# Transposing the small groups of the first head through VectorE and DRAM, with their scores further ahead

## The chip, the cores and the metric

The kernel runs on one core of a Trainium2 chip. The metric is the device time of one execution in microseconds (us); the kernel before takes 527.57 us, the median of three runs (525.86 to 528.05). The names of the engines in the rows are those of the profile: PE is TensorE's matmul side and PEld its weight load, DVE is VectorE, ACT is ScalarE, POOL is GpSimd, SP is SyncE (here only a DMA issuer; its queue is written SPq).

## The reference

One decoder layer on x of 1024 tokens by 1024 channels. Three mixers share one input projection: pooling, stick-breaking attention with 8 heads of 64, and softmax attention into 256 memory tokens. The change lies in the second:

```python
h = rmsnorm(x, norm_g)
proj = einsum('bsd,de->bse', h, w_in)          # pool_v, pool_gate, sb_q, sb_k, sb_v, sb_gate, mem_q, mem_gate
# stick-breaking attention, per head, for each block of 128 queries with L = the keys up to its end
z = einsum('bqhd,bkhd->bhqk', qb, kb) * scale
log_beta    = log_sigmoid(z)
log_1m_beta = where(mask, log_sigmoid(-z), 0)
cum  = cumsum(log_1m_beta, axis=-1)
a    = where(mask, exp(log_beta + cum[..., -1:] - cum), 0)
out  = einsum('bhqk,bkhd->bqhd', a, vb)        # then multiplied by silu(sb_gate)
# all groups concatenated, times w_out, plus x
```

## The kernel before, in words

Everything is computed in fp32 quality from products of high and low parts: an operand is rounded to a high part, the low part is the rest, and a product of two operands takes three matmuls (the calls that `unit_half` writes at L251 and L254). The projection is cut into units of 128 output channels: a unit is 16 steps of three 128x512 matmuls each. The units are the *fill*: matmuls that depend on nothing in the attention.

The stick-breaking attention is cut into 32 *groups* (p, j, h): p is one of four pairs of heads, j one of four stretches of 256 queries, and h the head of the pair, 0 (the first head) or 1. Group (p, j, h) sees 256(j+1) keys, that is 256, 512, 768 or 1024. Its keys are taken in j+1 *chunks* of 256; all groups make 80 chunks, numbered e = 0 to 79 in the order p, j, h. A pair of heads has 20 chunks.

For each group the kernel does this:

- `qk`: per block i of 128 queries, matmuls into a PSUM bank `z` (L754), a sigmoid on ACT into an SBUF tile `be` (L760, in pieces of up to 512 keys), then `scan`: a running product over the reversed row on DVE (L769). What comes out needs to be transposed, keys to partitions, before it can meet V.
- The transpose has two forms, chosen by `by_dma[n]`. Where it is false, `hl` calls `a_t`: four 128x128 transposes on PE into PSUM (L593, three for a group's last chunk, whose first half of the keys lies after the first 128 queries), the high part by ACT (L597) and the low part by DVE, which reads PSUM and the high part (L598). Where it is true, DVE transposes blocks of 32x32 in place right behind the scan (L771), four DMAs on SP's queue write the blocks to a DRAM tile `zd`, each block to its transposed place (L779), `rd` reads a chunk back three places ahead of its use (L799, or L804 and L805 for the last chunk of a group), and `hl` splits it: high part by ACT (L824), low part by POOL (L825), both from SBUF.
- `av`: four matmuls per chunk (L611) with the high and the low part against V, and at a group's end `av_out` on ACT (L630) and DVE (L633, L634).

Before the change the groups with h = 1 go through DRAM, and those with h = 0 through PE.

The order on every engine is written out by hand. `sb_slots` puts one `av` at each place e; at the same place stand `rd(e + 3)`, `hl(e + 1)` and the `qk` steps that a table gives. The scores of a couple of groups (p, j, 0) and (p, j, 1) are spread evenly over a window of places `c0` to `c1`, the second head first. `weave` then mixes the places with the fill in proportion, by planned PE times; `soon` puts an instruction that many planned microseconds later. The 80 places are cut in four parts, each woven with its own fill: the first with 48 fill steps and places up to e = 8, then e = 9 to 28, 29 to 48, and 49 to 79. The last part has 80 fill steps, and the pooling mixer's vector work (L927, L941 to L952) is written between them; the pooling needs DVE for its window sums and POOL for its low parts. This part is called the last stage below.

The `be` tiles rotate through four buffers, and for the first 58 tiles through two more (`Y0`, `Y1`). The tiles `al` have four buffers, `ah` two, and each PSUM bank name two.

Of the kernel before, what the change touches and what calls it, by code (L numbers as in the profile page):

```python
# [27 lines left out]
def layer_kernel(  # L28
# [707 lines left out]
    def sb_slots():  # L736
        groups = [(p, j, h) for p in range(4) for j in range(NT // 2) for h in range(2)]
        chunks = [(n, b) for n, (p, j, h) in enumerate(groups) for b in range(j + 1)]
        first = [chunks.index((n, 0)) for n in range(len(groups))]
        by_dma = [h == 1 for _, _, h in groups]  # L740
        be, zd, wt, acc, stored, n_be = {}, {}, {}, {}, [], [0]

        def qk(n, i, c):
# [99 lines left out]
        def qk_steps(n):  # L843
            p, j, h = groups[n]
            out = []
            for i in range(2):
                L = (2 * j + i + 1) * P
                for c in range((L - 1) // 512, -1, -1):
                    w = min(512, L - c * 512)
                    out.append((0.93e-3 * w, lambda i=i, c=c: qk(n, i, c)))  # L850
            return out


        slots = {}
        for n in range(0, len(groups), 2):
            c0, c1 = (first[n - 2] if n else -4) - 3, first[n] - 3
            for m, (lo, hi) in ((n + 1, (c0, (c0 + c1) / 2)), (n, ((c0 + c1) / 2, c1))):
                qs = qk_steps(m)
                for x, st in enumerate(qs):
                    slots.setdefault(int(lo + x * (hi - lo) / len(qs) // 1), []).append(st)  # L860
# [287 lines left out]
    def y_load():  # L1148
# [13 lines left out]
        )  # L1162
    )
    attn = sb_slots()
    weave(attn[0], fill_0)
    weave(attn[1], chain([u_q[2], u_k[2], u_g[2], u_v[2]], u_q[3]))
# [227 lines left out]
```

## Time and profile before

| what | value |
|---|---|
| median of 3 runs | 527.57 us (525.86 to 528.05) |
| profiled execution, its own time | 528.35 us |
| span in that profile, first to last instruction | 526.2 us |
| mean granted TensorE clock | 0.983 |
| PE busy | 499.3 us, 95% of the span |
| DVE busy | 403.4 us, 77% |
| ACT busy | 300.6 us, 57% |
| POOL busy | 248.2 us, 47% |

The first scores of the stick-breaking attention start on PE at 138.42 us, the last `av` matmuls at 419.76 us. From 437 us on the output projection runs. In a row of instructions in time order the columns are the start, the duration (of all merged instructions together, where xcount is above 1), engine, line, operation, and the tiles; behind them, in brackets, the idle time just before and what ended it. In the rows by groups the columns are the busy time, the mean of one instruction in ns, and the idle time before it. In the rows by stretches each engine has its busy time with the number of instructions, and then come the granted clock and the DMA engines' share.

### The profile page before, as it was taken

The page shows a single profiled execution, that of the slowest core. Times are in us where ns is not written, and L with a number is a line of the kernel's source. Part 1 is how long each engine was busy: PE and PEld are TensorE (multiplying, and loading weights), DVE is VectorE, ACT ScalarE, POOL GpSimd, SP SyncE. Part 2 cuts the span into 40 slices and gives each one's busy share as a digit, 9 for nine tenths or more (in the row PEclk, how much of TensorE's full clock was granted, in tenths as well). Part 3 has the DMA queues.
Part 4 walks back from the last instruction along what each step waited for, and adds up shares of the span by engine and source line. Part 5 has one row for each costly group of instructions (what it writes and reads, how often), then busy time and mean ns, then how long its engine had stood idle before and what let it go on. Part 6 is the DMA issues. An engine that isn't in the chain of part 4 may idle for free.

```text
span 526.2 us, 7899 instructions
## 1 busy us (share of the span) xinstructions
PE 499.3 (95%) x2548; PEld 416.4 (79%) x2548; DVE 403.4 (77%) x621; ACT 300.6 (57%) x676; POOL 248.2 (47%) x239
## 2 busy tenths in 40 slices
PE   7889999999999999999999999997878969999997
PEld 6678888888888788888888888885767848888886
DVE  4777777877379975699665998499993469999973
ACT  6877757778348654676556665564463438462400
POOL 4580335355124453544735348462474772055791
PEclk9999999999999999999999999998989978999999
DMA  8911111533537744665755756635445217323123
GB/s 308 333 40 41 30 52 40 119 85 79 127 80 154 152 101 107 149 131 116 146 125 148 141 123 140 150 70 130 124 87 159 80 53 229 120 81 124 35 105 135
DMA packets 150080, 62.45 MB, mean 119 GB/s; under 512 B 104070, under 2 KB 139160, under 8 KB 150040
## 3 DMA queue, kind: packets, MB, share of 16 engines
q1 hardware_dynamic: 150040, 61.96, 45.9%
q8 instruction: 20, 0.33, 0.3%
q14 instruction: 20, 0.16, 0.1%
HBM read 40.97 MB, written 16.78 MB: 110 GB/s over the span
## 4 chain that ended last, share of the span: by engine, by line
PE 70%; DVE 11%; ACT 6%; issue 4%; POOL 4%; DMA 3%; SPq 1%; DVEq 0%; POOLq 0%; ACTq 0%
PE av L611 6%; PE u_q L254 6%; PE u_k L254 5%; PE u_g L254 5%; DVE be L769 5%; PE u_v L254 4%; PE z L754 4%; PE u_q L251 3%; PE oS L1274 3%; PE oS L1276 3%; PE oS L1275 3%; PE u_k L251 3%; PE u_g L251 2%; PE u_pv L254 2%; PE oA L1274 2%
## 5 line engine op out<-in xcount | busy, mean ns | idle before, releaser
L769 DVE TENSOR_TENSOR_SCAN be<-be,later 128x128 f32<-128x128 f32 (+3 forms) x64 | 97.8, 1533 | 15.0 <-ACT be L760 14.8
L825 POOL TENSOR_TENSOR al<-al,ah 128x512 fp32r<-128x512 f32 (+1 forms) x40 | 61.4, 1537 | 44.0 <-ACT ah L824 40.2
L760 ACT ACTIVATE be<-z 128x128 f32<-128x128 f32 (+3 forms) x96 | 47.0, 491 | 41.7 <-PE z L754 31.1
L611 PE MATMUL av<-al,V_v 128*128 128x256 f32 (+1 forms) x160 | 32.8, 287 | 8.0 <-DVE al L598 6.1
L597 ACT ACTIVATE ah<-ta 128x512 fp32r<-128x512 f32 (+1 forms) x40 | 22.2, 554 | 30.7 <-PE ta L593 22.9
L598 DVE TENSOR_TENSOR al<-ta,ah 128x512 fp32r<-128x512 f32 (+1 forms) x40 | 25.2, 630 | 17.1 <-ACT ah L597 15.4
L611 PEld LDWEIGHTS av<-ah,V_v 128*128 128x128 f32 x160 | 29.9, 190 | 8.5 <-PE z L754 1.0
L611 PEld LDWEIGHTS av<-al,V_v 128*128 128x128 f32 x160 | 24.6, 192 | 9.5 <-DVE al L598 7.4
L611 PE MATMUL av<-ah,V_v 128*128 128x256 f32 (+1 forms) x160 | 30.5, 272 | 0.9 <-PE z L754 0.6
L703 POOL TENSOR_SCALAR pe_m<-pe_m,nb_m 128x256 f32<-128x256 f32 x16 | 16.8, 1053 | 27.8 <-DVE nb_m L700 24.1
L630 ACT ACTIVATE avt<-av,ve_v 64x128 f32<-64x128 f32 x64 | 19.8, 357 | 17.6 <-PE av L611 9.5
L754 PE MATMUL z<-KA_k,qa_q 128*128 128x512 f32 (+3 forms) x96 | 25.7, 352 | 2.7 <-ACT be L760 2.7
L824 ACT ACTIVATE ah<-al 128x512 fp32r<-128x512 f32 (+1 forms) x40 | 23.4, 584 | 6.8 <-DMA al<-zd 3.8
L251 PE MATMUL u_g<-hh,wh_g 128*128 128x512 f32 x64 | 26.5, 415 | 0.0
L251 PE MATMUL u_v<-hh,wh_v 128*128 128x512 f32 x64 | 26.3, 411 | 0.0
L251 PE MATMUL u_k<-hh,wh_k 128*128 128x512 f32 x64 | 26.2, 410 | 0.0
L1274 PE MATMUL oS<-bs,hh 128*128 128x512 f32 (+1 forms) x68 | 25.9, 380 | 0.0
L1276 PE MATMUL oS<-bs,hl 128*128 128x512 f32 (+1 forms) x68 | 25.8, 379 | 0.0
L771 DVE STREAM_TRANSPOSE be<-be 128x128 f32<-128x128 f32 (+7 forms) x32 | 24.9, 779 | 1.1
L754 PE MATMUL z<-KB_k,qb_q 128*128 128x512 f32 (+3 forms) x96 | 25.7, 350 | 0.0
L1275 PE MATMUL oS<-bs,hh 128*128 128x512 f32 (+1 forms) x68 | 25.6, 377 | 0.0
L692 ACT ACTIVATE pe_m<-z_m,nb_m,qsc 128x256 f32<-128x256 f32 x32 | 17.8, 561 | 13.5 <-DVE nb_m L688 11.0
(322 smaller groups left out, 1579.1 us busy)
## 6 DMA issues: line engine op xcount, KB each, us to landing
al<-zd SPq DMA_DIRECT2D x24, 256.0 KB, 2.9
x<-in_x_dram SPq DMA_DIRECT2D x8, 512.0 KB, 6.2
wr_q<-in_w_in_dram SPq DMA_DIRECT2D x4, 512.0 KB, 3.7
wr_k<-in_w_in_dram SPq DMA_DIRECT2D x4, 512.0 KB, 4.8
wr_v<-in_w_in_dram SPq DMA_DIRECT2D x4, 512.0 KB, 3.9
KA_k<-KA_k SPq DMA_DIRECT2D x8, 256.0 KB, 3.5
KB_k<-KB_k SPq DMA_DIRECT2D x8, 256.0 KB, 3.7
wr_g<-in_w_in_dram SPq DMA_DIRECT2D x4, 512.0 KB, 3.8
```

The source lines that it names most:

```text
L251: nc.tensor.matmul(pt[:], wh[:, kc], hh[k][:, c], start=(k == 0), stop=False)
L254: nc.tensor.matmul(pt[:], w[:, kc], h[k][:, c], start=False, stop=(k == KD - 1 and n == 1))
L598: low = lambda: nc.vector.tensor_tensor(al[:, :w], tp[:, :w], f(ah[:, :w]), op=ALU.subtract)
L611: nc.tensor.matmul(av[:, 256 - bw : 256], vs[n], part[:, o : o + bw], start=(first and part is ah and n == 0), stop=(last and part is al a ...
L754: nc.tensor.matmul(zp[:, 0:w], q[h][:, tcol], k[h][:, m, s0 : s0 + w], start=(m == 0), stop=(m == 1))
L760: nc.scalar.activation(t[:, s0 : s0 + w], zp[:, 0:w], AF.Sigmoid, scale=-(HD**-0.5))
L769: nc.vector.tensor_tensor_scan(t[:, rev], t[:, rev], mask, 1.0, op0=ALU.mult, op1=ALU.max)
L771: nc.vector.transpose(t[:, 0:L], t[:, 0:L])
L825: nc.gpsimd.tensor_tensor(lo[:, 0:w], f(lo[:, 0:w]), f(hi[:, 0:w]), op=ALU.subtract)
L1274: nc.tensor.matmul(bk[:, c], xh[:, tcol], wh[:, c], start=(n == 0), stop=False)
L1275: nc.tensor.matmul(bk[:, c], xh[:, tcol], wl[:, c], start=False, stop=False)
L1276: nc.tensor.matmul(bk[:, c], xl[:, tcol], wh[:, c], start=False, stop=(n == 3))
```

## The change

The groups of the first head with j = 0 and j = 1 (256 and 512 keys) now also have `by_dma` true. So that their stores reach DRAM before `rd` wants them, the scores of these couples end 6 places ahead of the group's first `av`, instead of 3. The windows now join: each begins where the one before it ends, so that the couple j = 0 has a window of 5 places instead of 8, j = 1 keeps 2, j = 2 has 7 instead of 4, and j = 3 keeps 6. The first of all begins at place -12 instead of -7, so that the first part is spread over 21 places instead of 16.

```diff
         first = [chunks.index((n, 0)) for n in range(len(groups))]
-        by_dma = [h == 1 for _, _, h in groups]
+        by_dma = [h == 1 or j < 2 for _, j, h in groups]
...
         slots = {}
+        c1 = -12
         for n in range(0, len(groups), 2):
-            c0, c1 = (first[n - 2] if n else -4) - 3, first[n] - 3
+            c0, c1 = c1, first[n] - (6 if by_dma[n] else 3)
             for m, (lo, hi) in ((n + 1, (c0, (c0 + c1) / 2)), (n, ((c0 + c1) / 2, c1))):
```

Eight groups change their form (two for each of the four pairs of heads), with 12 chunks. Behind the changed line the line numbers of the kernel are higher by one.

How the order moves, at three places of the last pair of heads. In the names, `be_3_1_2_0` is the score tile of pair 3, head 1, query block 2 (so j = 1); the last number is a buffer's. A line of "..." stands where rows are left out. First PE behind the `av` of chunk 60, where the transposes for chunk 62 stand, the first chunk of the first head's group of 512 keys. Before:

```order
L611 MATMUL av_41_4048<-al_60_3998,V_v3_3652 128x128
L251 MATMUL u_pg1_1_3946<-hh6_91,wh_pg1_3740 128x512
...
L754 MATMUL z_3_0_4_1_4064<-KA1_k3_3139,qa1_q3_2980 128x128 x2
L593 MATMUL ta_62_4069<-ident_69,be_3_0_2_0_3958 128x128
L593 MATMUL ta_62_4069<-ident_69,be_3_0_3_0_3973 128x128
...
L251 MATMUL u_pg1_1_3946<-hh7_92,wh_pg1_3740 128x512
```

And after the change, behind the same `av` of chunk 60:

```order
L611 MATMUL av_41_4130<-al_60_4000,V_v3_3689 128x128
L251 MATMUL u_pg1_1_4073<-hh5_90,wh_pg1_3789 128x512
L254 MATMUL u_pg1_1_4073<-hl5_98,wh_pg1_3789 128x512
L254 MATMUL u_pg1_1_4073<-hh5_90,wl_pg1_3790 128x512
L754 MATMUL z_3_0_5_0_4153<-KA1_k3_3233,qa1_q3_3015 128x512 x2
L251 MATMUL u_pg1_1_4073<-hh6_91,wh_pg1_3789 128x512
```

The transposes into `ta_62` are gone (two of its four are shown), and the scores at this point belong to a later query block; the fill around them is the same.

Second DVE in the same stretch, at the scores of j = 1 (query blocks 2 and 3); the scans (L769) are listed here under the name SCALAR_TENSOR_TENSOR. Before:

```order
L633 TENSOR_TENSOR av_39_3784<-av_39_3784,avt_2_0_3_3877 64x256
...
L927 TENSOR_TENSOR us1_3738<-us1_3738 128x511
...
L769 SCALAR_TENSOR_TENSOR be_3_1_2_0_3915<-be_3_1_2_0_3915,later_147 128x384
L771 STREAM_TRANSPOSE be_3_1_2_0_3915<-be_3_1_2_0_3915 128x384
...
L769 SCALAR_TENSOR_TENSOR be_3_1_3_0_3937<-be_3_1_3_0_3937,later_147 128x512
...
L769 SCALAR_TENSOR_TENSOR be_3_0_2_0_3958<-be_3_0_2_0_3958,later_147 128x384
L769 SCALAR_TENSOR_TENSOR be_3_0_3_0_3973<-be_3_0_3_0_3973,later_147 128x512
...
L598 TENSOR_TENSOR al_60_3998<-ta_60_3993,ah_60_3997 128x384
L769 SCALAR_TENSOR_TENSOR be_3_1_4_1_3991<-be_3_1_4_1_3991,later_147 128x640
```

And now:

```order
L769 SCALAR_TENSOR_TENSOR be_3_1_2_0_3882<-be_3_1_2_0_3882,later_147 128x384
...
L769 SCALAR_TENSOR_TENSOR be_3_1_3_0_3906<-be_3_1_3_0_3906,later_147 128x512
...
L769 SCALAR_TENSOR_TENSOR be_3_0_2_0_3925<-be_3_0_2_0_3925,later_147 128x384
L771 STREAM_TRANSPOSE be_3_0_2_0_3925<-be_3_0_2_0_3925 128x384
L769 SCALAR_TENSOR_TENSOR be_3_0_3_0_3940<-be_3_0_3_0_3940,later_147 128x512
L771 STREAM_TRANSPOSE be_3_0_3_0_3940<-be_3_0_3_0_3940 128x512
L633 TENSOR_TENSOR av_39_3840<-av_39_3840,avt_2_0_3_3946 64x256
...
L769 SCALAR_TENSOR_TENSOR be_3_1_4_1_3967<-be_3_1_4_1_3967,later_147 128x640
...
L928 TENSOR_TENSOR us1_3787<-us1_3787 128x511
```

The four scans of j = 1 now stand ahead of the end of group (2, 3, 0) (`av_39`) and of the first window sum of the pooling, where they stood behind both; the first head's two have their own 32x32 transposes, and the low part of chunk 60 is no longer DVE's.

Third POOL, chunks 59 to 65. Before:

```order
L825 TENSOR_TENSOR al_59_3889<-al_59_3889,ah_59_3967 128x384
L278 TENSOR_TENSOR wl_pg0_3926<-wr_pg0_3854,wh_pg0_3925 128x256
L825 TENSOR_TENSOR al_61_3952<-al_61_3952,ah_61_4035 128x384
...
L825 TENSOR_TENSOR al_64_4062<-al_64_4062,ah_64_4153 128x512
L825 TENSOR_TENSOR al_65_4102<-al_65_4102,ah_65_4174 128x384
```

And now:

```order
L825 TENSOR_TENSOR al_59_3961<-al_59_3961,ah_59_4038 128x384
...
L825 TENSOR_TENSOR al_60_4000<-al_60_4000,ah_60_4083 128x384
L278 TENSOR_TENSOR wl_pg0_4060<-wr_pg0_3957,wh_pg0_4059 128x256
L825 TENSOR_TENSOR al_61_4035<-al_61_4035,ah_61_4110 128x384
...
L825 TENSOR_TENSOR al_62_4071<-al_62_4071,ah_62_4150 128x512
L825 TENSOR_TENSOR al_63_4107<-al_63_4107,ah_63_4189 128x384
L825 TENSOR_TENSOR al_64_4142<-al_64_4142,ah_64_4212 128x512
L825 TENSOR_TENSOR al_65_4177<-al_65_4177,ah_65_4234 128x384
```

The low parts of chunks 60, 62 and 63 have come to POOL, so that it now has every chunk from 56 to 65.

## The prediction

> **What bounds the kernel now.** I read the page's first part, then the stretches of the span, then who PE waited for, and last the chain of waits.
>
> ```profile
> PE 499.3 (95%) x2548; PEld 416.4 (79%) x2548; DVE 403.4 (77%) x621; ACT 300.6 (57%) x676; POOL 248.2 (47%) x239
> 138.00:340.00 202.00, 200.85 (x1065) 170.03 (x1064) 154.13 (x191) 119.91 (x275) 92.30 (x85) 1.00 0.59 130
> 320.00:340.00 20.00, 20.00 (x113) 17.03 (x112) 11.96 (x18) 11.10 (x26) 11.71 (x12) 1.00 0.76 166
> 340.00:360.00 20.00, 18.33 (x100) 15.38 (x99) 18.31 (x20) 11.02 (x30) 13.83 (x12) 1.00 0.37 80
> 360.00:380.00 20.00, 16.49 (x81) 13.23 (x81) 19.58 (x24) 9.79 (x24) 5.36 (x3) 0.91 0.55 136
> 380.00:400.00 20.00, 14.84 (x70) 12.03 (x69) 15.08 (x18) 9.97 (x21) 13.91 (x10) 0.91 0.57 130
> 400.00:420.00 20.00, 20.00 (x110) 16.93 (x108) 9.40 (x15) 9.21 (x23) 9.90 (x11) 1.00 0.32 99
> ```
>
> Columns of the stretches: length, then busy us of PE, PEld, DVE, ACT and POOL, the granted clock, the DMA share. Two regimes lie in the attention. From 138 to 340 us PE is busy for 200.85 of 202 us: whatever PE is spared there is time. From 340 to 400 us PE is busy for 18.33 + 16.49 + 14.84 = 49.7 of 60 us, and DVE fills 18.31 and 19.58 of its 20. So 10.3 us of PE are lost there, and the clock falls to 0.91 over 31.3 us of PE work (16.49 + 14.84), another 31.3 x 0.09 = 2.8 us: 13 us in all to be won, at most, in the last stage.
>
> ```profile
> PE av L611 <- DVE al L598: 5.1, 3, 3.5
> PE z L754 <- ACT be L760: 2.7, 3, 1.7
> PE av L611 <- POOL al L825: 1.7, 2, 1.3
> 345.91 0.97 DVE be L769
> ...
> 350.79 0.83 DVE ps L927
> 351.62 3.30 DVE be L769 x2
> 354.92 0.58 DVE ps L927
> 355.50 0.47 DVE al L598
> 355.97 1.75 DVE be L769
> 357.74 0.86 DVE be L771
> ...
> 399.44 0.69 DVE L598 TENSOR_TENSOR al<-ta,ah 128x512 fp32r<-128x512 f32 x1 [4.61 <-ACT ah L597]
> ```
>
> The first three rows are PE's waits from 340 to 420 us (total, times, longest). Most of them are for DVE's low part `al`, which is short but stands in DVE's queue behind scans and window sums. The next are from the chain of waits: DVE runs from one item to the next without a gap, so it is a backlog on DVE, not one slow item, that PE meets. The last row, from DVE in order of time, is its first long pause: 4.61 us before 399.44, so the run goes from 345.9 to 394.8 us.
>
> **The change part by part.** *PE is spared its transposes.* Per pair of heads the chunks of j = 0 and 1 take 3 + 4 + 3 = 10 of them, 40 in all.
>
> ```profile
> 398.28 0.44 PE ta L593 x4
> 337.46 0.33 PE ta L593 x3
> ```
>
> On the chain four cost 0.44 us and three 0.33, so 0.11 each: 40 x 0.11 = 4.4 us. Thirty lie in the regime where PE is the bound: **-3.3 us**, nothing beside them. The ten of the last pair are worth **-1.1 us** only where PE is on the path again; I count them, with a bound of 0.
>
> *DVE loses the low parts and gains 32x32 transposes.*
>
> ```profile
> L598 DVE TENSOR_TENSOR al<-ta,ah 128x512 fp32r<-128x512 f32 x24 | 16.4, 684 | 12.4 <-ACT ah L597 10.9 <-issue 1.1
> L598 DVE TENSOR_TENSOR al<-ta,ah 128x384 fp32r<-128x384 f32 x16 | 8.8, 549 | 4.7 <-ACT ah L597 4.5
> 140.43 0.31 DVE L771 STREAM_TRANSPOSE be<-be 128x128 f32<-128x128 f32 x1
> 146.08 0.45 DVE L771 STREAM_TRANSPOSE be<-be 128x256 f32<-128x256 f32 x1
> L771 DVE STREAM_TRANSPOSE be<-be 128x384 f32<-128x384 f32 x1 | 0.6, 579 | 0.0
> L771 DVE STREAM_TRANSPOSE be<-be 128x512 f32<-128x512 f32 x1 | 0.7, 711 | 0.0
> ```
>
> Per pair: out 0.684 + 2 x 0.549 = 1.78 us, in 0.31 + 0.45 + 0.58 + 0.71 = 2.05 us. That is +0.27 us per pair, covered by PE before 340 us (DVE is busy 154.13 of 202).
>
> *POOL gets the 12 low parts.*
>
> ```profile
> L825 POOL TENSOR_TENSOR al<-al,ah 128x512 fp32r<-128x512 f32 x24 | 38.9, 1621 | 35.3 <-ACT ah L824 31.6 <-PE av L611 2.2 <-DMA al<-zd 1.5
> L825 POOL TENSOR_TENSOR al<-al,ah 128x384 fp32r<-128x384 f32 x16 | 22.6, 1412 | 8.7 <-ACT ah L824 8.6
> 149.11 0.69 DVE L769 TENSOR_TENSOR_SCAN be<-be,later 128x256 f32<-128x256 f32 x1 [0.30 <-ACT be L760]
> 340.97 1.29 POOL L825 TENSOR_TENSOR al<-al,ah 128x512 fp32r<-128x512 f32 x1
> 341.04 1.78 DVE L769 TENSOR_TENSOR_SCAN be<-be,later 128x256 f32<-128x256 f32 x1 [2.13 <-ACT be L760]
> ```
>
> POOL's own time is 1.62 + 2 x 1.41 = 4.44 us per pair, 17.8 in all, on an engine busy for 92.30 of 202 us. The dearer part is what it does to DVE. A scan of 256 keys takes 0.69 us alone and 1.78 us where a POOL low part began just before it: 1.09 us more; it ends at 342.82, POOL's part at 342.26. DVE's low part from PSUM shows no such stretching (mean 0.684). So each moved low part may cost DVE up to 1.09 us, three of them in the last stage up to 3.3 us; the lower bound is 0, where POOL's part meets a DVE item that it does not stop. [...]
>
> *DMAs.* 16 more score tiles are stored, in 64 DMAs, and the 12 chunks are read back in 20, all on SP's queue.
>
> ```profile
> L779 SPq DMA_DIRECT2D zd<-be x128: 302/493/2589, 140.9 to 384.7; - x128
> al<-zd SPq DMA_DIRECT2D x24, 256.0 KB, 2.9
> ```
>
> At the median of 0.49 us the issues take 84 x 0.49 = 41 us of SP over some 280 us. Behind a store that waits for DVE stand the reads `rd` and the weight loads; they are late next if DVE lags. A read lands 2.9 us after its issue and is issued three places ahead, about 9 us, so I take 0, with an upper bound of 1.5 us (one issue-and-landing overrun at the densest place, j = 1, where 16 stores stand within two places).
>
> *The scores move ahead.* In the first part the places shrink. It ran from the first scores to the first fill of the next part:
>
> ```profile
> 138.42 0.34 PE L754 MATMUL z<-KB_k,qb_q 128*128 128x128 f32 x2
> 188.40 0.45 PE L251 MATMUL u_q<-hh,wh_q 128*128 128x512 f32 x1
> ```
>
> That is 50 us for 16 places, 3.1 us each; with 21 places and 1.1 us less, 2.3 us each. An `av` then follows every 2.3 us, and a low part on POOL (1.4 to 1.6 us plus a weight quarter now and then) still fits, though with little to spare: I take **+1 us** of new PE waits, between 0 and 3.
>
> In the last stage the gain is larger. The four scans of j = 1 leave the backlog:
>
> ```profile
> L769 DVE TENSOR_TENSOR_SCAN be<-be,later 128x512 f32<-128x512 f32 x2 | 3.8, 1899 | 0.0
> L769 DVE TENSOR_TENSOR_SCAN be<-be,later 128x384 f32<-128x384 f32 x2 | 2.7, 1359 | 0.4 <-ACT be L760 0.4
> ```
>
> 3.8 + 2.7 us with their two old transposes (0.58 + 0.71) and the three low parts (1.78) make 9.6 us of DVE work that no longer lies in the run of 345.9 to 394.8 us. They go to 320 to 345 us, where DVE is busy for 11.96 of 20 us and so has 8 us free (from the row of 320 to 340). Against that stand up to 3.3 us of stretching by POOL, and the j = 2 scans that come up to three places earlier and start the run sooner: the lag at its end falls by 9.6 - 3.3 = 6 us, perhaps 2 to 9. PE does not get all of it, since some of the 13 us hang on the j = 3 scores and the pooling's POOL work, which stay. I take two thirds, **-4 us**, between 0 and -9.
>
> Sum: -3.3 - 1.1 + 1 - 4 = -7.4 us. The profiled execution took 528.35 us (a span of 526.2 and 2.15 around it), 0.78 above the median of 527.57. So 528.35 - 7.4 = 520.95, and by the median 527.57 - 7.4 = **520.2 us**.
>
> **The rivals.** *Only PE's own part shows.* The last stage ends where the j = 3 scores and the pooling let it; nothing is won or lost there, and the first part costs nothing: 527.57 - 3.3 = 524.3 us. For it: the longest wait (3.5 us for `al` L598) belongs, by its place in PE's order, to a group of j = 2, whose low part stays on DVE. Against it: DVE has run without a gap for 40 us by then, so what is taken out ahead of it must show.
>
> *Nothing changes.* The last stage gives back what PE was spared before it: its end is set by DVE and POOL, which get +0.27 and +4.44 us of work in this pair, while PE only arrives 3.3 us earlier and waits longer: about 527.5 us. For it: DVE's 19.58 of 20 us. Against it: the work that moves out is fixed to places of PE's order, which arrive earlier too.
>
> *POOL becomes what `av` waits for* (slower). All chunks of j = 0 and 1 now need POOL, which also makes the fill's low weights, and DVE's scans stop it. The trace has two such waits, 1.7 us, 0.85 each. If each of the 12 moved chunks waited so long, that is 10.2 us against 4.4 of PE and no relief: 527.57 + 5.8 = 533.4 us. It decides from 4.4 / 12 = 0.37 us per chunk on. [...] Against it: with two `ah` buffers POOL has two places of time for each, 4.6 us, and before the change the ten chunks per pair that take this way cost PE 1.7 us in all.
>
> **How the numbers follow.** The forecast has 0.57, only PE's part 0.17, nothing 0.13, POOL 0.13. The forecast's own range is -3.3 - 1.1 - 9 = -13.4 to -3.3 + 3 - 0 = -0.3, so 514 to 527; its middle is likelier than its ends. To hold 8 in 10 it must take in the second case and touch the third: 514 to 527.8 us. What a measurement of this kernel can tell is about 0.5%, 2.6 us: faster means below 524.9. That is nearly all of the forecast (0.54) and most of the second case (0.14), together 0.68. Slower is the last case but for its mild end, 0.11. The rest is 0.21.
>
> **What would show it.** PE should keep its 200.85 of 202 us where it is the bound, with the group L593 into `ta` at 104 instead of 144, and the next pairs should start earlier, by 1.1 us per pair. In the first part, waits of `av` for POOL's `al` above 3 us would show that the places are too short. In the last stage PE's idle time should fall from 10.3 us to about 6 or 7 and the clock stay nearer to 1.00; DVE should be busier from 320 to 340 us than 11.96, and the mean of L825 should not rise much above 1.62 and 1.41. The prediction is wrong if PE's waits for `al` in the last stage stay at 6.8 us (5.1 + 1.7) or move whole to POOL, or if SP's stores hold up the reads so that ACT waits for `al<-zd`.

## The result, and the profile after

The changed kernel takes 524.83 us (median of 20 runs, 522.28 to 530.58) beside 527.92 us for the kernel before (median of 20 runs, 525.86 to 530.79): a ratio of 0.994, with a 95% interval of 0.9922 to 0.9957. It is faster by 3.1 us, where 7.4 was forecast. The same kernel run once more with other kernels, as below, gave 523.48 us and a ratio of 0.9919 (0.9897 to 0.9941), so the gain is 3 to 4.5 us. The profiled execution took 522.64 us with a span of 520.9.

The engines' busy time on the page of the kernel after, then the group of the transposes, then the stretches, with the columns as in the prediction:

```profile
PE 493.8 (95%) x2508; PEld 411.4 (79%) x2508; DVE 411.3 (79%) x625; ACT 301.1 (58%) x676; POOL 273.3 (52%) x251
```

```profile
L593 PE MATMUL ta<-ident,be 128*128 128x128 f32 x104 | 15.9, 272 | 0.0
```

```profile
138.00:340.00 202.00, 197.04 (x1026) 165.71 (x1026) 162.10 (x197) 119.32 (x274) 108.59 (x93) 1.00 0.69 146
320.00:340.00 20.00, 20.00 (x114) 17.23 (x115) 15.23 (x21) 10.57 (x27) 11.53 (x10) 1.00 0.70 138
340.00:360.00 20.00, 18.49 (x96) 15.29 (x94) 19.73 (x21) 11.82 (x30) 16.21 (x13) 1.00 0.75 161
360.00:380.00 20.00, 16.71 (x88) 13.75 (x89) 19.20 (x26) 12.21 (x29) 8.78 (x8) 1.00 0.68 160
380.00:400.00 20.00, 16.47 (x80) 13.52 (x79) 15.14 (x18) 10.12 (x22) 15.71 (x11) 0.91 0.52 142
```

The 40 transposes are gone. From 138 to 340 us, where PE was busy for all but 1.15 us, it now idles for 5 (202 - 197.04). In the last stage DVE takes up work before 340 us (15.23 for 11.96), PE is busy 51.7 of the 60 us from 340 to 400 instead of 49.7, and the clock is 1.00 for 20 us longer (the last section shows that this differs between executions of one kernel).

To see where the time went I cut the attention at instructions that both kernels have: the first score product, the first fill product of each next part, and the last `av`. Their rows in PE's time order, first before, then after:

```profile
255.41 0.39 PE L251 MATMUL u_q<-hh,wh_q 128*128 128x512 f32 x1
322.46 0.39 PE L251 MATMUL u_pv<-hh,wh_pv 128*128 128x512 f32 x1
419.76 0.39 PE L611 MATMUL av<-al,V_v 128*128 128x256 f32 x2
```

```profile
137.93 0.34 PE L754 MATMUL z<-KB_k,qb_q 128*128 128x128 f32 x2
190.34 0.44 PE L251 MATMUL u_q<-hh,wh_q 128*128 128x512 f32 x1
257.03 0.39 PE L251 MATMUL u_q<-hh,wh_q 128*128 128x512 f32 x1
323.97 0.39 PE L251 MATMUL u_pv<-hh,wh_pv 128*128 128x512 f32 x1
416.04 0.39 PE L611 MATMUL av<-al,V_v 128*128 128x256 f32 x2
```

| us | first part | second | third | last stage |
|---|---|---|---|---|
| before | 49.98 | 67.01 | 67.05 | 97.30 |
| after | 52.41 | 66.69 | 66.94 | 92.07 |
| difference | +2.43 | -0.32 | -0.11 | -5.23 |
| forecast | -1.1 + 1 = -0.1 | -1.1 | -1.1 | -4 - 1.1 = -5.1 |

The differences make -3.2 us. That this comes so near to the 3.1 of the medians is partly luck, since the profiled execution of the kernel after lies 2.2 us below its median. The two profiled executions differ by more (528.35 - 522.64 = 5.7), because the one before also took 0.5 us longer to its first score product and 1.4 longer from the last `av` to the output projection. (The output projection's first product starts at 445.50 us in the kernel before, not at 437.) Without the change in the last pair that stretch was 25.74 us, and 24.45 and 25.37 in two runs below; with it, it was 23.5 to 25.0. A gain of some tenths there is possible and not shown, and I do not count it. The parts are from one execution each; between the kernel after and its repeat below they differ by up to 0.7 us, so medians stand beside them.

What PE waited for, by part, in the kernel after: the first three rows are the first part, then one row for the second, two for the third, and four from 340 to 420 us.

```profile
PE av L611 <- DVE al L598: 1.7, 1, 1.7
PE av L611 <- POOL al L825: 1.4, 2, 1.1
PE z L754 <- ACT be L760: 0.2, 1, 0.2
...
PE av L611 <- DVE al L598: 0.8, 1, 0.8
...
PE av L611 <- DVE al L598: 0.6, 1, 0.6
PE av L611 <- POOL al L825: 0.2, 1, 0.2
...
PE av L611 <- DVE al L598: 4.3, 2, 2.8
PE av L611 <- DVE g_g L634: 2.6, 1, 2.6
PE av L611 <- POOL al L825: 0.9, 2, 0.8
PE z L754 <- ACT be L760: 0.4, 1, 0.4
```

In the first part of the kernel before, PE waited once, 1.0 us; in the second and third not at all. The waits of PE's weight loads (PEld), whose records overlap PE's, come out somewhat longer (1.9 us where PE's row has 1.7) and account for the parts more closely. In the first part, one row before and three after:

```profile
PEld av L611 <- DVE al L598: 1.1, 1, 1.1
```

```profile
PEld av L611 <- POOL al L825: 2.0, 3, 1.2
PEld av L611 <- DVE al L598: 1.9, 1, 1.9
PEld z L754 <- ACT be L760: 0.7, 1, 0.7
```

That is 4.6 us for 1.1, so 3.5 more; less the 1.1 spared it makes +2.4, and +2.43 was measured. In the second and third part the loads wait 1.0 and 1.2 us, where they waited 0.3 each: 0.7 and 0.9 of the 1.1 us are given back. So two questions stand: what gives the spared transposes back in the second and third part, and what makes the first longer.

### The profile page after: what moved, and what is told of

Same layout as the page of the kernel before. It is cut to its first block, busy times and chain, and to the rows that moved or that the text cites. A ratio compares the mean times of both kernels' runs of the same rounds, so it can differ in the third digit from the quotient of the medians.

```text
span 520.9 us, 8045 instructions
## 1 busy us (share of the span) xinstructions
PE 493.8 (95%) x2508; PEld 411.4 (79%) x2508; DVE 411.3 (79%) x625; ACT 301.1 (58%) x676; POOL 273.3 (52%) x251
## 4 chain that ended last, share of the span: by engine, by line
PE 62%; DVE 14%; ACT 7%; issue 5%; DMA 5%; SPq 4%; POOL 2%; DVEq 0%; ACTq 0%; POOLq 0%
DVE be L769 6%; PE u_q L254 6%; PE av L611 5%; PE u_v L254 3%; DMA al<-zd 3%; PE u_k L254 3%; PE u_mg L254 3%; SPq L779 3%; PE u_q L251 3%; PE oS L1275 3%; PE oS L1277 3%; PE oS L1276 3%; PE u_pv L254 3%; PE z L754 2%; PE oA L1277 2%
## 5 line engine op out<-in xcount | busy, mean ns | idle before, releaser
L769 DVE TENSOR_TENSOR_SCAN be<-be,later 128x128 f32<-128x128 f32 (+3 forms) x64 | 102.0, 1593 | 24.0 <-ACT be L760 22.7
L825 POOL TENSOR_TENSOR al<-al,ah 128x512 fp32r<-128x512 f32 (+1 forms) x52 | 75.5, 1454 | 35.5 <-ACT ah L824 20.5
L824 ACT ACTIVATE ah<-al 128x512 fp32r<-128x512 f32 (+1 forms) x52 | 30.0, 578 | 18.0 <-DMA al<-zd 12.9
L771 DVE STREAM_TRANSPOSE be<-be 128x128 f32<-128x128 f32 (+7 forms) x48 | 33.1, 690 | 1.6
L597 ACT ACTIVATE ah<-ta 128x512 fp32r<-128x512 f32 (+1 forms) x28 | 15.8, 566 | 21.9 <-PE ta L593 16.0
L598 DVE TENSOR_TENSOR al<-ta,ah 128x512 fp32r<-128x512 f32 (+1 forms) x28 | 18.1, 646 | 12.8 <-ACT ah L597 12.3
L254 PE MATMUL u_v<-hl,wh_v 128*128 128x512 f32 x64 | 25.3, 396 | 0.0
```

Source lines behind the costliest of these rows:

```text
L254: nc.tensor.matmul(pt[:], w[:, kc], h[k][:, c], start=False, stop=(k == KD - 1 and n == 1))
L769: nc.vector.tensor_tensor_scan(t[:, rev], t[:, rev], mask, 1.0, op0=ALU.mult, op1=ALU.max)
L771: nc.vector.transpose(t[:, 0:L], t[:, 0:L])
L824: nc.scalar.activation(hi[:, 0:w], f(lo[:, 0:w]), AF.Copy)
L825: nc.gpsimd.tensor_tensor(lo[:, 0:w], f(lo[:, 0:w]), f(hi[:, 0:w]), op=ALU.subtract)
```

## The experiments

Eighteen kernels were run, each beside the kernel before, whose median was 527.6 to 528.0 us throughout. Part times are taken as above, each from one profiled execution. In five of them one of the first two parts holds a stretch at half clock, which is named where it counts.

### The parts apart

Only the last pair of heads changed:

```diff
-        by_dma = [h == 1 or j < 2 for _, j, h in groups]
+        by_dma = [h == 1 or (j < 2 and p == 3) for p, j, h in groups]
...
-        c1 = -12
+        c1 = -7
```

> The change is made in the last pair of heads alone (p = 3: two more groups through DRAM, windows 3 places earlier there). In the traces the last stage (first matmul of its fill to the last av) fell from 97.7 to 92.5 us, 5.2 us. Theory A (the last stage won what was forecast, and the first part lost about 3.5 us of it again): the gain is all here, about -5 us, 522 to 523.5 us. Rival (only PE's own part shows; the last stage's 5.2 us is what one profile happened to show): the ten transposes alone, -1.1 us, 526 to 527.5 us.

Measured: 522.57 us, ratio 0.9892 (0.9871 to 0.9913); the parts are 49.99, 67.02, 67.05 and 93.94 us. The last pair alone wins more (5.5 us) than the whole change (3.1 to 4.5).

All pairs but the first changed (the same diff, with `p > 0`):

> The change is made in the pairs p = 1, 2, 3; the first pair keeps its form and its windows of before, from place -7. Theory A (the first part alone loses, 2.4 us where 1.1 were to be won): 2.4 us less than the whole change, 521 to 522.8 us. Rival B (the loss is spread: SP's queue or POOL in all parts): the first pair's ten transposes are missing and nothing is won by leaving it out: 525 to 526 us.

Measured: 521.31 us, 0.9873 (0.9848 to 0.9898); parts 49.97, 66.85, 67.18 and 91.80. Leaving the first part out is better than the whole change by 2 to 3.5 us. The second and third part win next to nothing here too. The whole change, run again without an edit:

> The changed kernel once more, unaltered, for its time beside the others on this chip and for a second trace. Its median of 20 runs is 524.8 us. If the parts of the trace are a property of the kernel: first part 52.4, second 66.7, third 66.9, last stage 92.5 us, each within 0.5 us. If the profile was a lucky one (522.64 us, 2.2 below the median), one of the parts comes out longer, and that is the part that decides.

Measured: 523.48 us; parts 52.43, 66.49, 66.52 and 92.79. The first part's loss repeats to 0.02 us.

### Why the second and third part keep so little

First the price of a transpose. In the kernel before, the 40 transposes are done twice:

```diff
             for src in b:
-                nc.tensor.transpose(tp[:, o : o + P], src, ident[:])
+                for _ in range(1 + twice):
+                    nc.tensor.transpose(tp[:, o : o + P], src, ident[:])
```

> The kernel before, with each of the 40 transposes of the first head's groups of 256 and 512 keys done twice on TensorE (the second writes the same values into the same place): the price of such a transpose by itself. If TensorE sets the end where they stand, 40 times 0.11 us, +4.4 us (3.3 for the 30 of the first three parts), spread as 1.1 us over each part: 531-533 us. If TensorE has room for them there: within 1 us of before. Each of the parts 2 and 3, 67.0 us before, should come to 68.1 by the one and stay at 67.0 by the other.

Measured: 531.27 us, 1.0072 (1.0053 to 1.0091). The rows of its parts in PE's time order:

```profile
137.97 0.34 PE L755 MATMUL z<-KB_k,qb_q 128*128 128x128 f32 x2
189.57 0.45 PE L251 MATMUL u_q<-hh,wh_q 128*128 128x512 f32 x1
257.67 0.39 PE L251 MATMUL u_q<-hh,wh_q 128*128 128x512 f32 x1
325.82 0.39 PE L251 MATMUL u_pv<-hh,wh_pv 128*128 128x512 f32 x1
422.50 0.39 PE L612 MATMUL av<-al,V_v 128*128 128x256 f32 x2
```

The second and third part take 68.10 and 68.15 us, 1.09 and 1.10 more than before: ten transposes at 0.11 us, exactly as priced. The first takes 51.60 (+1.62), the last 96.68 (0.62 less). So transposes count in full where PE is the bound, and nothing in the last stage of the kernel before, where PE idled 1.6 us less instead.

Next, the suspicion on POOL. The 12 low parts that the change brought to POOL are given to DVE:

```diff
-            nc.gpsimd.tensor_tensor(lo[:, 0:w], f(lo[:, 0:w]), f(hi[:, 0:w]), op=ALU.subtract)
+            (nc.gpsimd if groups[n][2] else nc.vector).tensor_tensor(lo[:, 0:w], f(lo[:, 0:w]), f(hi[:, 0:w]), op=ALU.subtract)
```

> The whole change, with the low parts of the weights that it newly brings through DRAM (12 subtractions, three in each part) taken by VectorE and not by GpSimd. If GpSimd's subtractions with two inputs in SBUF are what stretches VectorE's scans (L769, 97.8 us before, 102.0 with the change) and eats the 1.1 us that parts 2 and 3 should each have won: L769 back to 98-99 us, parts 2 and 3 at 66.0-66.4 instead of 66.7 and 66.9, time 522.5-524. If not: parts 2 and 3 as in the change, and the last stage gives back what three subtractions cost VectorE there, 1 to 2 us, so 524.5-526.5 us.

Measured: 523.79 us, 0.9924 (0.9901 to 0.9947); parts 52.10, 66.52, 66.43 and 94.46. The second and third part are those of the unedited repeat (66.49, 66.52), and the scans did not become shorter. The group of the scans, of the kernel after and of this one:

```profile
L769 DVE TENSOR_TENSOR_SCAN be<-be,later 128x128 f32<-128x128 f32 (+3 forms) x64 | 102.0, 1593 | 24.0 <-ACT be L760 22.7 <-DMA zd<-be 1.0
```

```profile
L769 DVE TENSOR_TENSOR_SCAN be<-be,later 128x128 f32<-128x128 f32 (+3 forms) x64 | 101.3, 1583 | 16.9 <-ACT be L760 16.6
```

101.3 us against 102.0, where 98 to 99 was expected. The last stage gives back 2.4 us (94.46 for 92.07, or for 92.79 in the repeat 1.7): three low parts return to the engine that is short there, and PE waits 1.8 us for one of them. POOL's low parts are not what eats the gain.

The wait itself points to the cause. DVE in order of time near the end of the second part of the kernel after, and then PE's row that waits for it:

```profile
246.40 2.27 DVE L769 TENSOR_TENSOR_SCAN be<-be,later 128x1024 f32<-128x1024 f32 x1
248.70 1.25 DVE L771 STREAM_TRANSPOSE be<-be 128x1024 f32<-128x1024 f32 x1
...
252.23 0.69 DVE L598 TENSOR_TENSOR al<-ta,ah 128x512 fp32r<-128x512 f32 x1
```

```profile
252.97 0.50 PE L611 MATMUL av<-al,V_v 128*128 128x256 f32 x2 [0.79 <-DVE al L598]
```

The low part that PE waits for belongs to the second chunk of the first head's 768-key group, which still goes by PE. On DVE it stands behind the scan and the 32x32 transposition of 1024 keys. Each of the three parts has this wait at this place. The next edit lets that transposition wait, so that the low part goes first:

```diff
                 nc.vector.tensor_tensor_scan(t[:, rev], t[:, rev], mask, 1.0, op0=ALU.mult, op1=ALU.max)
-                if by_dma[n]:
-                    nc.vector.transpose(t[:, 0:L], t[:, 0:L])
...
             soon(1.0, scan)
             if by_dma[n]:
+                soon(1.0 + (2.3 if L == 1024 else 0.0), lambda: nc.vector.transpose(t[:, 0:L], t[:, 0:L]))
```

> The whole change, and on VectorE the transposition of the 1024-key scores stands no longer right behind their scan but behind the low part of the next chunk of the first head's 768-key group, which so comes 1.25 us earlier. Theory C (in each part TensorE hands the 1.1 us that the transposes spared back in one wait, 1.7, 0.8 and 0.6 us, for that low part, which stands on VectorE behind the scan and the transposition of 1024 keys): the three waits go, part 1 from 52.4 to 50.5-51.2, parts 2 and 3 from 66.7 and 66.9 to 65.9-66.2 us; 520.5-522.5 us in all. Rival D (the spared transposes were never on the path, or another wait takes the place): parts 2 and 3 stay within 0.3 us of 66.7 and 66.9, 523-525 us.

Measured: 523.21 us, 0.9924 (0.9899 to 0.995); parts 54.00, 65.68, 66.22 and 93.62. In the second and third part theory C came out: 1.0 and 0.7 us won. In the first it did not: the named wait went from 1.7 to 0.4 us, and a new one of 1.9 for the next low part came behind it.

The same edit on the kernel whose first part is as before:

> The same edit of VectorE's order on the kernel that leaves the first part as before and changes the three others (521.3 us). Theory C: parts 2 and 3 from 66.85 and 67.2 to 65.9-66.2 us, and the 1.0 us wait of the first part may stay; 519-520.5 us. Rival D: 521-522 us.

Measured: 519.25 us, 0.984 (0.982 to 0.986); parts 49.93, 66.10, 65.96 and 92.61. This is the fastest kernel of the study, 8.7 us below the kernel before. The same place in its second part, DVE and then PE:

```profile
244.09 2.27 DVE L769 TENSOR_TENSOR_SCAN be<-be,later 128x1024 f32<-128x1024 f32 x1
...
248.65 0.69 DVE L598 TENSOR_TENSOR al<-ta,ah 128x512 fp32r<-128x512 f32 x1
249.26 1.23 DVE L784 STREAM_TRANSPOSE be<-be 128x1024 f32<-128x1024 f32 x1
```

```profile
249.54 0.39 PE L611 MATMUL av<-al,V_v 128*128 128x256 f32 x2
```

The low part now comes first, and PE's row carries no wait. And the same edit on the kernel before (there with 3.2 for 2.3, which puts the low part first):

> The same edit of VectorE's order on the kernel before, where TensorE waits for that low part in no part but the last. Theory C: parts 2 and 3 stay at 67.0 us, since TensorE is full there, and the time stays within 1.5 us of before; only the last part can move. If it wins 2 us or more in parts 2 and 3, the order helps without the change and theory C does not say why the change won so little there.

Measured: 527.39 us, 0.9981 (0.9966 to 0.9996); parts 49.93, 66.68, 66.79 and 96.81. The edit is worth 0.3 us per part without the change and 0.75 to 1.2 with it (66.85 to 66.10, 67.18 to 65.96). A part of the same code differs by up to 0.8 us between profiles, but the groups do not meet: with the change and DVE's old order the second and third part take 66.4 to 67.2 us in nine profiles, with the edit 65.7 to 66.2 in four (leaving out one part that lost 1.7 us to the clock). So the two belong together: PE was spared 1.1 us per part, and most of it went into a wait at one place where DVE's order was made for a slower PE.

### Why the first part grows

The prediction named places that are too short, and SP's stores. Both were tried first by giving the places ahead of the first `av` 7/12 of their fill, so that the later ones are as long as before:

```diff
-            (e, [Step(us, fn, (most + 0.1 - sum(u for u, _ in st)) / len(st)) for us, fn in st]) for e, st in out
+            (e, [Step(us, fn, max(0.0, (most + 0.1) * (7 / 12 if e < 0 else 1) - sum(u for u, _ in st)) / len(st)) for us, fn in st])
+            for e, st in out
```

> The whole change, but the places before the first av get 7/12 of the weight in the mix with the fill, so that the first av comes after 22.0 us of PE's work instead of 28.3 and the av places of the first part last 3.1 us again instead of 2.3. Theory A (the places of 2.3 us are too short for DVE's j = 3 scores and for read, split and low part of a chunk): the first part wins back about 3 us, 521 to 522.5 us, and PE's waits there fall from 3.4 to under 1 us. Rival B (SP's queue, with 32 store DMAs ahead of the first reads, holds up weight loads and reads): the stores now come in a shorter stretch, so no gain: 524.5 to 526 us, with reads of al still late.

Measured: 524.84 us, 0.9934 (0.9911 to 0.9957); the first part 53.72 us. The `av`s came early, at 21.7 us instead of 28.4, but PE then stood for 2.55 us: ACT held a sigmoid back because it waited 5.38 us, in order, for a read that SP issued only at 160.87 us, behind 28 stores. Of the 53.72 us, 3.1 are a clock at half that followed this pause (last section), so the part time says little against the pacing itself; the median shows no gain from it. The long wait spoke for SP's queue, so the stores were tried alone, on the kernel that leaves the first part as before, with nothing that reads them (`dummy` is the loop of four stores, to a DRAM tile of its own):

```diff
             else:
                 stored.append((n, i))
+                if p == 0 and j < 2:
+                    soon(3.4 + 3.8e-3 * L, lambda: dummy(n, i, t, L))
```

> The kernel that leaves the first part as before (PE transposes there) and changes the three others, 521.3 us, plus one thing: in the first part the scores of the first head's groups of 256 and 512 keys are also stored to DRAM, 16 stores on SP's queue at the places where the changed kernel has them, and nothing reads them. Theory A (the first part loses because SP's queue, which issues in order, carries 16 more stores ahead of the weights' loads and the reads): the first part, from the first score product to the next part's first fill product, grows from 49.97 us to 51.5-53, the time to 523-525 us. Rival B (what costs is the new chain itself: the transposed weights come late because their scores start too late): nothing reads the stores, so the first part stays at 50.0 and the time at 521-522 us.

Measured: 521.18 us, 0.988 (0.9857 to 0.9903); the first part 49.99. Theory A in this form falls: 16 more stores alone cost nothing. Then the other way round, the whole change with those 16 stores on ACT's queue:

```diff
-                    nc.sync.dma_start(
+                    (nc.scalar if p == 0 and h == 0 else nc.sync).dma_start(
```

> The whole change, with the 16 new stores of the first part issued from ACT's queue and not from SP's; reads and all else as in the change. Theory A (SP's queue): SP's other loads and reads come on time again, the first part falls from 52.4 us to 50-51, the time to 521.5-523 us. Rival B (the chain of scan, transposition, store and read is too long for the places it has, whichever queue issues it): the first part stays at 52-53, the time at 523.5-525. A third outcome, that ACT's own waits for VectorE's transpositions hold up its sigmoids, would show as PE waiting for ACT in the first part and over 525 us.

Measured: 522.69 us, 0.9908 (0.9883 to 0.9933); the first part 51.14. Here SP's queue does matter, for 1.3 of the 2.4 us by the profile and 0.8 to 2.1 by the medians, whose intervals overlap. PE's weight loads now wait 0.9 us for POOL's low parts instead of 2.0; the 1.9 for DVE's and 0.6 for ACT's sigmoid stay. Stores alone did not hurt (49.99 us with 16 more, 49.97 without); stores ahead of reads with little slack did (52.41 us with the 16 on SP's queue, 51.14 with them on ACT's). In the kernel after, SP carries 16 stores in 11.33 us ahead of the gate's weights, and ACT waits five times for a read; before, not once in this part. SP's rows in time order, and ACT's wait from 138 to 192 us:

```profile
140.39 11.33 SPq L779 DMA_DIRECT2D zd<-be  x16
151.81 0.40 SPq L152 DMA_DIRECT2D wr_g<-in_w_in_dram  x1
```

```profile
ACT ah L824 <- DMA al<-zd: 4.4, 5, 1.4
```

Both remedies together:

> The whole change, VectorE's order edited as above, and the first part's 16 new stores issued from ACT's queue. If the first part's loss is the sum of two causes, SP's queue (1.3 us, as the run with ACT's queue showed) and the low part behind VectorE's 1024-key work (1.7 us of waiting), it falls to 49.3-50 us, no longer than before; time 519.5-521.5. If the two are one wait seen twice, it stays at 51 us.

Measured: 523.27 us, 0.9908 (0.9883 to 0.9933); parts 52.26, 68.56, 65.82 and 93.06. The causes do not add: as in the run with DVE's order alone, a wait of 1.9 us for the next low part takes the place, here just behind the cut, in the second part, and a clock at half behind it costs that part 1.7 us more. This profile is the slowest of six executions (525.51 us), but the median of 523.27 does not add up either.

Next, whether ACT's holds starve DVE. DVE idles for 2.87 us before 176.38 in the kernel after, and is full from 180 us on. ACT's copies are put behind the scores of their place:

```diff
-            steps = a + qs[: len(qs) // 2] + b + qs[len(qs) // 2 :]
+            k = len(qs) if e < 19 and by_dma[chunks[e + 1][0]] else len(qs) // 2
+            steps = a + qs[:k] + b + qs[k:]
```

> The whole change, with ACT's copy of a chunk read from DRAM (and so GpSimd's subtraction) put behind the scores of its place and not in the middle of them, in the first part only: ACT, which works in order, no longer holds a sigmoid back while it waits for a read. Theory E (the first part loses by ACT's holds: 4.4 us of waiting for reads, the scores behind them late, VectorE without work for 2.9 us near 173 us and then too full, TensorE waiting 1.7 us for a low part): VectorE's gap shrinks below 1.5 us, the first part falls from 52.4 to 50.5-51.3 us, the time to 522-523.3. Rival F (VectorE's gap comes from the places: the first groups' scores were moved ahead and the later ones were not): the gap stays at 2.5 us or more, the first part at 52-53 us, 523.5-526 in all.

Measured: 524.42 us, 0.9925 (0.9901 to 0.9948); the first part 52.03, DVE's gap 3.58 us. The edit reaches up to place 18, so it also touches the second part (67.48 us). Theory E falls: PE's wait for the low part went from 1.7 to 0.7 us, but the gap behind it did not close. And whether DVE's gap comes from the later scores' places:

```diff
-            c0, c1 = c1, first[n] - (6 if by_dma[n] else 3)
+            c0, c1 = c1, first[n] - (6 if by_dma[n] or n < 8 else 3)
```

> The whole change, and in the first part the scores of the first head's groups of 768 and 1024 keys end six places ahead of their use too, not three, so that all of that part's scores after the first pair come earlier by three places. Rival F: VectorE's gap of 2.9 us near 173 us closes, TensorE's wait of 1.7 us for the low part goes, the first part falls from 52.4 to 50-51.2 us, the time to 521.5-523. Theory E: the reads and ACT's holds are as before, the first part stays at 52 us or more.

Measured: 523.57 us, 0.9913 (0.9882 to 0.9944); the first part 51.95. F's mechanism came out and its price did not: DVE's gap closed and PE's wait for the low part went, but a wait of 1.65 us for the end of an accumulator (`g_g`, L634) and one of 0.8 for POOL came instead. With less DRAM work in the first part, the 256-key group only:

```diff
-        by_dma = [h == 1 or j < 2 for _, j, h in groups]
+        by_dma = [h == 1 or (j < 2 and (p > 0 or j == 0)) for p, j, h in groups]
```

> The whole change, but in the first part only the group of 256 keys goes by VectorE and DRAM, the group of 512 keys stays with TensorE: 8 new stores on SP's queue in place of 16, one new chunk to read in place of three. If the loss of the first part follows the stores and reads: about half of it, a first part of 50.3-51.3 us, 522-523.3 in all. If it follows the earlier start of the scores, which this kernel keeps in part, it stays near 52 us; if it all hangs on the 512-key group: 49.5-50 us and 521-522.

Measured: 526.47 us, 0.9971 (0.9944 to 0.9998); the first part 55.47, with a wait of 2.9 us for a low part and one of 1.1 for an accumulator's end. Of the 55.47 us, 1.7 are a clock at half behind the longer wait. None of the three expectations came out. With half the stores and a third of the reads it is worse, so the loss does not simply grow with the DRAM work. (The edit also lets the scores of j = 1 end three places ahead again instead of six, so more than the DRAM work differs.) What this kernel keeps is the early start of the scores, and a later first `av`: 27.0 us behind the first score product (24.5 before, 28.4 after). The fill is fixed at 48 steps, so what lies ahead of the first `av` is missing between the `av`s that follow. That alone was tried on the kernel with the first part as before: 1.35 times the fill ahead of the first `av`, no other edit:

```diff
-            (e, [Step(us, fn, (most + 0.1 - sum(u for u, _ in st)) / len(st)) for us, fn in st]) for e, st in out
+            (e, [Step(us, fn, max(0.0, (most + 0.1) * (1.35 if e < 0 else 1) - sum(u for u, _ in st)) / len(st)) for us, fn in st])
+            for e, st in out
```

> The kernel that leaves the first part as before (521.3 us), with one thing changed: the places ahead of the first weight product get 1.35 times the fill, so that this product comes after 28.4 us of TensorE's work as in the changed kernel, not after 24.9, and the next nine places share 23.1 us in place of 26.6. No new store, read or VectorE work in the first part. Theory G (the change's additional places ahead of the first weight product take fill from those behind it, whose VectorE, ACT and GpSimd work then is too dense): the first part grows from 49.97 to 51.5-53 us with TensorE waiting for a low part or for an accumulator, 523-524.5 us in all. Rival E (late reads are the cause): no read is later, the first part stays at 50.0-50.5 and the time at 521-522.

Measured: 525.57 us, 0.9952 (0.9928 to 0.9976); the first part 53.62 and the second 68.21. The first `av` and PE's waits in the two parts:

```profile
166.38 0.34 PE L611 MATMUL av<-ah,V_v 128*128 128x256 f32 x2
```

```profile
PE av L611 <- DVE al L598: 2.7, 2, 2.0
PE av L611 <- DVE g_g L634: 0.3, 1, 0.3
...
PE av L611 <- DVE al L598: 1.4, 1, 1.4
```

With no new store, read or item on DVE, a first `av` 28.0 us behind the first score product (166.38 - 138.35; 24.5 without the edit) costs 4.3 us by the medians (525.57 - 521.31), and PE waits for low parts again. A clock at half behind the longest wait makes 1.0 us of the first part and 0.7 of the second, and this profile lies 1.5 us above its median. Theory G's mechanism is shown; the price is above the one it named. What it would give to take it away from the whole change, by starting nine places ahead:

```diff
-        c1 = -12
+        c1 = -9
```

> The whole change with the first pair's scores from nine places ahead and not twelve: the first weight product comes after 25.5 us of TensorE's work (28.3 in the change, 24.9 before), all the DRAM work stays. Theory G: the first part falls from 52.4 to 49.5-50.8 us, 521-522.5 in all. Rival E: the reads now have less time, the first part stays at 52-54 us, 523.5-525.5.

Measured: 527.14 us, 0.9978 (0.9953 to 1.0003); the first part 55.91. Worse, where theory G wanted better, and here the loads are late. SP's and ACT's rows:

```profile
140.66 17.79 SPq L779 DMA_DIRECT2D zd<-be  x28
...
159.53 0.38 SPq L152 DMA_DIRECT2D wr_g<-in_w_in_dram  x1
```

```profile
164.39 0.72 ACT L277 ACTIVATE wh_g<-wr_g 128x256 fp32r<-128x256 f32 x2 [2.56 <-DMA wr_g<-in_w_in_dram]
```

28 stores now stand ahead of the gate's weights, whose load is issued 7.7 us later than in the kernel after (159.53 for 151.81); ACT waits for it, and the sigmoids queue up behind. The first `av` comes at 28.3 us again, by waiting instead of by plan. With DVE's order edited as well:

> As the one before, with VectorE's transposition of 1024 keys behind the next low part as well. If theory G holds and parts 2 and 3 keep what that order won (66.0 us each): 519-521 us, no faster than the 519.3 of the kernel with the same order and the first part as before. If the first part still loses 2 us: 522-524.

Measured: 525.82 us, 0.9962 (0.9933 to 0.999); parts 54.26, 65.96, 66.12 and 92.87. The second and third part show theory C a third time; the first stays long (1.7 us of it are a clock at half). This profile is the fastest of twelve executions, 2.6 us below the median.

So the first part is bounded from two sides. It is the start of the attention, where nothing older keeps the engines going. The DRAM route needs its scores early, and early scores ahead of the first `av` take the fill from the places behind it, where DVE's low parts then come late (squeeze). With fewer places ahead, SP's queue holds up the weights and reads (start9, paced). I found no place between. How much of the 2.4 us is owed to each side is not settled: SP's queue is worth about 1.3 by the profile, and the remedies did not add up.

## Why the prediction was wrong

- **PE is spared its transposes: the price was right, the cover was not.** Ten cost 1.09 and 1.10 us in the parts that show it (the doubled transposes). Of the 2.2 us forecast for the second and third part 0.4 arrived (1.1 in the repeat). The step that failed is "nothing beside them" together with "covered by PE before 340 us (DVE is busy 154.13 of 202)": an average over 202 us, where one place per part decides. There a low part stands on DVE behind a scan and a transposition of 1024 keys, and PE, now 1.1 us earlier, meets it for 0.8 and 0.6 us. With that one item moved, the parts were 0.8 to 1.3 us shorter than in the kernel before.
- **The first part: the term was mis-sized, and it is the largest miss.** I took +1 us of waits for POOL, between 0 and 3, and 0 for the DMAs, up to 1.5; beside the spared 1.1 us that made -0.1, and +2.43 was measured: 2.5 of the 4.2 us by which the parts missed the forecast. The new waits of PE's weight loads are 3.5 us: 2.0 for POOL's low parts, 0.8 for DVE's and 0.7 for ACT's sigmoids. POOL was the right engine, but not only for the reason given: with the new stores on ACT's queue its share fell to 0.9 and the part by 1.3 us, so much of it came through SP's queue, which I had set at 0. "A read ... is issued three places ahead, about 9 us" used the old length of a place. The waits for DVE, counted as covered, and for ACT were not in the sum at all. How the rest divides between the short places and the early start stays open.
- **The last stage: right in sum, the mechanism in part, and some luck.** -5.23 us measured, -5.1 forecast; the profiles of kernels with the change in the last three pairs, low parts on POOL, have 91.8 to 93.6 us there, those of the kernel before and its two variants 96.7 to 97.3, so the gain is 3 to 5.5. DVE's work moved to 320 to 340 us as said (15.23 us for 11.96), and PE's waits for `al` from 340 us on fell from 6.8 to 5.2 us, but a new one of 2.6 for an accumulator's end (`g_g`, L634) came. PE's idle time from 340 to 400 us fell from 10.3 to 8.3, not to 6 or 7. The clock gave another 1.5 us (it cost 3.2 us of PE's work before and 1.7 after, an estimate from the granted clock), and this is chance in one execution. Whether the last ten transposes won their 1.1 is not settled: doubled, they made that stage no longer. Nor did a run separate the earlier scores from the changed form.
- **DVE and POOL.** L825's means are 1523 and 1375 ns, not above the 1621 and 1412 of before, as the forecast wanted. The scans took 4.2 us more in all (102.0 for 97.8), 0.35 us per moved low part, where the bound was 1.09. The third rival has DVE's scans stop POOL; the trace of before shows it at 254.40 us: the scan of 1024 keys took 2.29 us, and the low part of 128x512 that began 0.03 us behind it took 3.35, where the next one of that shape, at 257.86 with no scan beside it, took 1.30. With the 12 low parts taken from GpSimd the scans' sum hardly moved (101.3), so these runs do not show that those low parts stretched them, and the second and third part did not get shorter.
- **The rivals.** "Only PE's own part shows" was 524.3 us, and 524.83 was measured, but that is luck: the last stage won, which it excluded, and most of PE's own part did not show. "POOL becomes what `av` waits for" came in the first part alone: PE waited 1.4 us for it there and 0.2 in the next two together.

Of the signs that would make the prediction wrong, the one on SP's stores came true: ACT waited 4.4 us for `al<-zd` in the first part, five times.

## What to carry to other kernels

Time spared on the bounding engine is kept only where the next engine's item is ready that much earlier; look for the one place per period where its order is tight, not at its average load, and mend the order with the change. Here the change with DVE's order mended and the first period left out won 8.7 us, the whole change alone 3.1 to 4.5. A route with a longer latency (in the kernel after, a read of 256 KB from `zd` landed 3.0 us after its issue, in the median) needs a head start, and at the beginning of a phase the head start is paid from the same fill that covers what follows: leave the first period as it is and change the rest.

## What the hardware showed

A short pause of PE cost more than its length here. In the run with 7/12 of the fill ahead of the first `av`, PE stood still for 2.55 us up to 164.67, and its granted clock then fell to a half. The stretches of that run (length; busy time of PE, PEld, DVE, ACT and POOL; clock; DMA share):

```profile
162.00:164.00 2.00, 0.12 (x1) 0.00 (x0) 1.10 (x2) 0.40 (x1) 0.00 (x0) 1.00 0.85 154
164.00:166.00 2.00, 1.33 (x3) 1.15 (x4) 1.35 (x1) 1.96 (x5) 1.00 (x1) 0.52 0.22 41
166.00:168.00 2.00, 2.00 (x8) 1.72 (x8) 1.92 (x3) 1.55 (x5) 1.17 (x2) 0.50 0.70 165
168.00:170.00 2.00, 2.00 (x6) 1.52 (x6) 1.12 (x3) 1.52 (x4) 1.28 (x2) 0.50 0.78 132
170.00:172.00 2.00, 2.00 (x8) 1.61 (x7) 2.00 (x1) 1.06 (x4) 1.57 (x2) 0.77 0.77 182
```

From 164.67 to about 171 us PE ran at half speed, so the pause of 2.55 us cost about 3 more (6 us at 0.5).

The length of the pause does not decide it alone. In the kernel after, PE pauses for 2.65 us up to 361.30 us, and the clock stays at 1.00 for the next 8 us; after its pause of 2.75 us up to 383.32 the clock is 0.50 from 383.5 to 386.9 us. In the kernel before, a shorter pause of 1.66 us up to 362.68 and one of 0.64 up to 364.14 come ahead of a clock of 0.50 from 365.1 to 368.5 us. The wait of 1.7 us in the first part of the kernel after left the clock at 1.00; one of 1.97 us in the run with 1.35 times the fill, up to 188.44, was followed by products 0.43 us apart instead of 0.23 from 189.9 to 193.3 us, which is about half speed. A stretch of 3.4 us at 0.5 costs about 1.7 us. In the last stage the kernel before has two of them (the second from 385.6 to 389.0 us), the kernel after the one named, and the fastest kernel, by an estimate from its mean clock of 0.992, none. Over the 20 runs of the kernel after, the mean clock lies between 0.974 and 0.993, so a part time from a single profile holds this chance.
